# Ordering a hybrid attention and delta-rule block with another scheduler clock, from an inner context

## The chip, the cores and the metric

The kernel runs on one core of a Trainium2 chip, as one launch. The metric is the device time of that core in microseconds (us), and the lower one is better. A change is judged by the ratio of its time to that of the kernel before, measured in turns on the same chip.

The core has five engines that work side by side, each through a queue of its own, in order: PE (TensorE, the matmuls; its weight loads are a row of their own, PEld), DVE (VectorE), ACT (ScalarE), POOL (GpSimd) and SP (SyncE, which here issues nearly all DMAs).

## The reference

One layer of an encoder trunk, for two sequences of 256 and 512 rows with 1024 features. The input is normed and multiplied by one wide weight matrix; the product is cut into the inputs of two branches. One branch is attention with a difference of two softmaxes for each of 8 heads, the other a gated delta rule in both directions, in chunks of 64 in the reference. Gates merge the two, and a last matmul and norm follow. Cut to what matters:

```python
def trunk(x, norm_g, w_in, conv_w, lam_qk, diff_norm_g, a_log, dt_bias, gdn_norm_g, w_branch, w_out, final_g):
    h = rmsnorm(x, norm_g[l])
    proj = h @ w_in[l]
    q_a, k_a, v_a, z_a, qkv_b, z_b, a_b, b_b, gate = jnp.split(proj, SPLIT_POINTS, -1)
    y_a = diff_branch(q_a, k_a, v_a, z_a, lam_qk[l], diff_norm_g[l], lam_init, cos, sin)
    y_b = gdn_branch(qkv_b, z_b, a_b, b_b, conv_w[l], a_log[l], dt_bias[l], gdn_norm_g[l])
    gates = jax.nn.sigmoid(gate.astype(jnp.float32)).astype(x.dtype).reshape(B, S, 2, D)
    merged = gates[:, :, 0] * (y_a @ w_branch[l, 0]) + gates[:, :, 1] * (y_b @ w_branch[l, 1])
    x = x + merged @ w_out[l]
    return rmsnorm(x, final_g)

# attention branch: w = softmax(q1 k1) - lam * softmax(q2 k2); o = w @ v; rmsnorm; times silu(z)
# delta rule, for each direction and head, over chunks i:
    t = lax.linalg.triangular_solve(a + eye, eye, lower=True, unit_diagonal=True)   # a = strict(beta k k^T * decay)
    v_new = u_i - w_i @ state
    o = qg_i @ state + attn_i @ v_new
    state = state * gl_i + kd_i^T @ v_new
```

## The kernel before

Both sequences stand side by side, 768 columns in 6 chunks of 128. Values are float32; the large matmuls run with operands split into a high and a low part (`whi` and `wlo` for weights), so that each product is three matmuls.

*The weight stream.* The products with `w_in` and `w_branch` are cut into units of 128 output features. `load_split` (L155) loads a unit's weights on SP's queue (L157) into one of two buffers `raw` and splits them, on ACT (L152) and DVE (L153). The unit's body does 48 matmuls of 256 and 512 columns into `pa` and `pb` (L200) and then its epilogue: a convolution for the inputs of the delta rule (L394 to L408), a rotation for those of attention (L796 to L822), or a tanh for gates and z (L241 to L244, L289 to L291). `stream` (L185) hands out these matmuls in small steps.

*The work around it.* Four pairs of heads go through the delta rule (`gdn_pair`, L431): transposes of `kq` with norms (L448 to L464), values (L539, L540), decays (`decays`, L499: a gate, spread over a matrix, is summed by matmuls with a triangle, L526, and goes through an exp and a mask on POOL, L529), the inverse of the triangles (`inverse`), and six rounds of the scan, where DVE's `r` (L697) is the operand of the matmul at L708. Eight heads of attention follow, with a rope rotation, scores (L885), weights and a product with the values; each head ends in `finalize` (L295), with a power on POOL (L302), a scaling on DVE (L303) and transposes (L310). The last stages are the two branch products and `out_proj` (L990), which ends with the norm of each block of rows and its store (L1005 to L1014).

*What sets the order.* All of this is traced in one `TileContext`. Each traced instruction has a priority, counted up as it is traced. The weight stream is traced at priorities from 1000000 on, behind all else, except where a `fill` call asks for steps inline; `fill` calls also say how far the stream is traced at a point of the foreground. When the context closes, a list scheduler goes through the instructions with a simulated machine as its clock: at each point in that machine's time it gives each engine the ready instruction with the first priority, and that order becomes the engine's queue. Tile buffers are given out and semaphore waits are placed by the same pass. So the clock decides what counts as ready, and with it where the stream's matmuls stand between those of the foreground. The context before takes its time from the scheduler's default machine. All this happens while the kernel is built; on the chip each engine goes through its queue as it is.

`kernel` (L1096) opens the context and calls `tile_trunk` (L45), which holds all that is told above; L1110 is the line of the context's opening.

Of the kernel before, what the change touches and what calls it, by code (L numbers as in the profile page):

```python
# [41 lines left out]


@with_exitstack
def tile_trunk(  # L45
    ctx: ExitStack,
    tc: tile.TileContext,
    x_prompt, x_sample, norm_g, w_in, conv_w, lam_qk, diff_norm_g, a_log, dt_bias,
# [1027 lines left out]
    hes.close()  # L1076


# [1 line left out]
_INS = ["x_prompt", "x_sample", "norm_g", "w_in", "conv_w", "lam_qk", "diff_norm_g", "a_log", "dt_bias",  # L1080
        "gdn_norm_g", "w_branch", "w_out", "final_g"]
# [32 lines left out]
```

## Time and profile before

| | |
|---|---|
| median of 3 runs | 1220.1 us (1218.69 to 1220.44) |
| the profiled execution, its own time | 1219.2 us |
| its span, from the first to the last instruction | 1217.1 us |
| PE busy | 1186.3 us (97% of the span), 8015 matmuls |
| DVE, ACT, POOL busy | 754.4, 556.3, 132.0 us |
| mean granted clock of PE | 0.996 |

The profile is that of one execution. Its times are in us unless ns is said, counted from the first instruction; L12 is line 12 of the kernel; `out<-in` names the tile that an instruction writes and those that it reads. A granted clock of 1.00 is 2.4 GHz and one of 0.50 is 1.2 GHz. Matmuls are pipelined, so that neighbouring ones overlap in the list, and their ends are modelled. Idle time of an engine is put down to what ended it.

### The profile page before, as it was taken

How to read it: one execution, taken by the hardware profiler on the slowest of the kernel's cores; microseconds unless marked ns; L12 is line 12 of the kernel's file. 1: busy time of each engine (PE TensorE's matmuls, PEld its weight loads, DVE VectorE, ACT ScalarE, POOL GpSimd, SP SyncE). 2: the span in 40 equal slices, each digit the busy share in tenths (PEclk: the TensorE clock that was granted, in tenths of full speed). 3: DMA queues.
4: the chain of work that ended last, by engine and by line, in shares of the span. 5: the costliest groups of instructions: out<-in, count | busy, mean ns of one | idle time of the engine just before them, and what ended most of it. 6: DMA issues, size and time to landing. Idle time of an engine off the chain costs nothing. (4 is left out here: it accounts for less than half of the span.)

```text
span 1217.1 us, 20985 instructions
## 1 busy us (share of the span) xinstructions
PE 1186.3 (97%) x8015; PEld 1043.3 (86%) x8015; DVE 754.4 (62%) x1555; ACT 556.3 (46%) x1422; POOL 132.0 (11%) x242
## 2 busy tenths in 40 slices
PE   6999999999999999999999999999999999999997
PEld 5888889888888889888899889898898888888886
DVE  5778938667566855768354756767476645566332
ACT  6553546524672346722452545656365454332111
POOL 2132004301321013210000000000000000000000
PEclk9999999999999999999999999999999999999999
DMA  5123321244204340143425545353544548443131
GB/s 180 36 55 77 89 58 49 78 113 91 57 19 122 93 105 18 53 116 116 98 83 163 149 118 140 104 135 87 139 117 117 145 153 258 142 156 117 65 104 69
DMA packets 170647, 127.26 MB, mean 105 GB/s; under 512 B 53066, under 2 KB 147508, under 8 KB 170548
## 3 DMA queue, kind: packets, MB, share of 16 engines
q1 hardware_dynamic: 170416, 125.88, 37.2%
q8 instruction: 63, 1.03, 0.4%
q14 instruction: 36, 0.29, 0.1%
q10 hardware_dynamic: 132, 0.05, 0.0%
HBM read 83.43 MB, written 23.59 MB: 88 GB/s over the span
## 5 line engine op out<-in xcount | busy, mean ns | idle before, releaser
L200 PE MATMUL pb<-hT,whi 128*128 128x512 f32 x1152 | 430.8, 400 | 0.4 <-ACT hT L145 0.4
L200 PE MATMUL pa<-hT,whi 128*128 128x256 f32 x1152 | 317.3, 288 | 1.9 <-DVE gsp L243 1.9
L200 PEld LDWEIGHTS pb<-hT,whi 128*128 128x128 f32 x1152 | 216.1, 189 | 45.1 <-ACT hT L145 0.8
L200 PE MATMUL pb<-hT,wlo 128*128 128x512 f32 x576 | 228.9, 397 | 0.0
L200 PEld LDWEIGHTS pa<-hT,whi 128*128 128x128 f32 x1152 | 214.7, 190 | 6.3 <-DVE gsp L243 2.2
L152 ACT CAST whi<-raw 128x1024 fp32r<-128x1024 f32 x88 | 92.7, 1054 | 215.6 <-PE pb L200 206.5
L200 PE MATMUL pa<-hT,wlo 128*128 128x256 f32 x576 | 164.6, 286 | 0.0
L153 DVE TENSOR_TENSOR wlo<-raw,whi 128x1024 fp32r<-128x1024 f32 x88 | 107.7, 1224 | 78.1 <-ACT whi L152 77.9
L200 PEld LDWEIGHTS pb<-hT,wlo 128*128 128x128 f32 x576 | 108.7, 189 | 22.7
L200 PEld LDWEIGHTS pa<-hT,wlo 128*128 128x128 f32 x576 | 109.1, 189 | 1.5
L200 PE MATMUL pv<-vhi,hT 128*128 128x256 f32 x384 | 73.4, 287 | 0.3 <-ACT xp L796 0.3
L890 ACT ACTIVATE pw<-ps_sc,st 128x512 f32<-128x512 f32 (+1 forms) x96 | 58.2, 619 | 32.0 <-DVE st L888 31.9
L302 POOL TENSOR_TENSOR oss<-oss,mhalf 128x6 f32<-128x6 f32 x16 | 23.1, 1445 | 422.5 <-DVE oss L301 422.5
L404 DVE SCALAR_TENSOR_TENSOR kq<-xp,pcol,kq 128x258 f32<-128x258 f32 x96 | 56.2, 639 | 19.2 <-ACT kq L400 19.1
L200 PEld LDWEIGHTS pv<-vhi,hT 128*128 128x128 f32 x384 | 61.1, 191 | 1.2 <-ACT xp L796 0.6
L888 DVE TENSOR_REDUCE st<-ps_sc 128x1 f32<-128x512 f32 (+1 forms) x80 | 51.4, 682 | 10.2 <-PE ps_sc L886 9.9
L200 PE MATMUL pv<-vlo,hT 128*128 128x256 f32 x192 | 54.9, 286 | 0.0
L578 DVE TENSOR_TENSOR inv<-inv 96x31 f32<-96x31 f32 (+15 forms) x124 | 41.9, 338 | 17.5 <-ACT inv L556 14.2
L200 PE MATMUL pb<-yh,wlo 128*128 128x512 f32 x128 | 50.5, 396 | 0.0
L200 PE MATMUL pb<-yh,whi 128*128 128x512 f32 x128 | 50.4, 394 | 0.0
L200 PE MATMUL pb<-yl,whi 128*128 128x512 f32 x128 | 50.3, 393 | 0.0
L1004 PE MATMUL po<-hT,mh 128*128 128x512 f32 (+1 forms) x156 | 46.1, 378 | 0.3 <-DVE gth L949 0.3
(296 smaller groups left out, 2248.3 us busy)
## 6 DMA issues: line engine op xcount, KB each, us to landing
raw<-in_w_in SPq DMA_DIRECT2D x72, 512.0 KB, 4.1
xx<-xp SPq DMA_DIRECT2D x64, 192.0 KB, 3.5
raw<-in_w_branch SPq DMA_DIRECT2D x16, 512.0 KB, 4.0
gtd<-gsp SPq DMA_DIRECT2D x16, 384.0 KB, 2.7
th<-xp SPq DMA_DIRECT2D x64, 96.0 KB, 2.9
gth<-gtd SPq DMA_DIRECT2D x16, 384.0 KB, 4.2
vraw<-in_w_in SPq DMA_DIRECT2D x4, 1024.0 KB, 5.6
wor<-in_w_out SPq DMA_DIRECT2D x16, 256.0 KB, 3.5
```

The costliest lines, as they stand in the source:

```text
L152: nc.scalar.copy(whi, raw)
L153: nc.vector.tensor_tensor(out=wlo, in0=raw, in1=whi.bitcast(F32), op=ALU.subtract)
L200: nc.tensor.matmul(out, l_, r_, start=st, stop=sp)
L302: nc.gpsimd.tensor_tensor(out=oss[:, 0, :], in0=oss[:, 1, :], in1=mhalf[:, :NCH], op=ALU.pow)
L404: nc.vector.scalar_tensor_tensor(out=dst[:, a:b], in0=xp[:, w + a:w + b], scalar=cw(w), in1=dst[:, a:b], op0=ALU.mult, op1=ALU.add)
L578: nc.vector.tensor_tensor(out=tmp[:, :n, :w], in0=L[:, j + 1:, j:j + 1].to_broadcast(shp), in1=X[:, j:j + 1, :w].to_broadcast(shp), op=ALU ...
L888: nc.vector.tensor_reduce(out=st[:, c, :G], in_=ps.rearrange("p (g s) -> p g s", g=G), axis=AX.X, op=ALU.max, negate=True)
L890: nc.scalar.activation(pw[:, c, S * g_:S * g_ + S], ps[:, S * g_:S * g_ + S], AF.Exp, bias=st[:, c, g_:g_ + 1], accum_out=sums[:, c, i:i + 1])
L1004: nc.tensor.matmul(ps[:, :c1 - c0], a[:, ts_], b[:, cs], start=f, stop=l)
```

## The change

The function that traces the trunk is renamed to `trunk`. A new `tile_trunk` opens a section of the outer context that is scheduled as one piece (`tile_critical`), opens a second `TileContext` in it with the option `schedule_with_timeline_sim`, and traces the trunk in this inner context. With the option, the scheduler's simulated machine is the framework's timeline model in place of the default one. The body of the trunk, its priorities, its buffers and the call in `kernel` are as they were; the decays are still summed by matmuls (L526). The whole diff:

```diff
--- before.py
+++ after.py
@@ -42,7 +42,7 @@
 
 
 @with_exitstack
-def tile_trunk(
+def trunk(
     ctx: ExitStack,
     tc: tile.TileContext,
     x_prompt, x_sample, norm_g, w_in, conv_w, lam_qk, diff_norm_g, a_log, dt_bias,
@@ -1076,6 +1076,11 @@
     hes.close()
 
 
+def tile_trunk(tc, *args):
+    with tc.tile_critical(), tile.TileContext(tc.nc, schedule_with_timeline_sim=True) as inner:
+        trunk(inner, *args)
+
+
 # ---- launch: one core; inputs and outputs as the reference has them ----
 _INS = ["x_prompt", "x_sample", "norm_g", "w_in", "conv_w", "lam_qk", "diff_norm_g", "a_log", "dt_bias",
         "gdn_norm_g", "w_branch", "w_out", "final_g"]
```

## Rows read from the trace of the kernel before

**Rows 1.** The page: PE's busy time and share; granted clock in 40 slices, in tenths.
```profile
PE 1186.3 (97%) x8015; PEld 1043.3 (86%) x8015; DVE 754.4 (62%) x1555; ACT 556.3 (46%) x1422; POOL 132.0 (11%) x242
...
PEclk9999999999999999999999999999999999999999
```

**Rows 2.** Busy time by stretches: start:end, length, engines, PEclk, DMA share, GB/s.
```profile
0.00:40.00 40.00, 29.45 (x152) 24.21 (x153) 22.62 (x44) 24.31 (x44) 7.28 (x30) 1.00 0.48 150
...
1200.00:1217.00 17.00, 10.17 (x68) 9.13 (x66) 5.15 (x12) 2.11 (x8) 1.10 (x2) 0.88 0.16 62
```

**Rows 3.** What PE waited for: us in total, times, longest.
```profile
PE ps_par L116 <- DMA prow<-in_diff_norm_g: 7.4, 1, 7.4
...
PE ps_t L448 <- DVE kq L408: 2.1, 1, 2.1
PE pa L200 <- DVE gsp L243: 1.9, 1, 1.9
PE ps_yt L310 <- DVE o L303: 1.7, 1, 1.7
PE ps_x L708 <- DVE r L697: 1.4, 1, 1.4
...
PE ps_v L539 <- DVE vT L408: 0.2, 1, 0.2
```

**Rows 4.** Busy time by stretches, behind the stalls at 69 and 870 us.
```profile
70.00:72.00 2.00, 2.00 (x10) 1.91 (x10) 0.00 (x0) 1.22 (x8) 0.00 (x0) 0.50 0.80 235
72.00:74.00 2.00, 2.00 (x12) 1.77 (x11) 0.17 (x1) 1.54 (x9) 0.00 (x0) 0.75 0.03 8
...
872.00:874.00 2.00, 2.00 (x10) 1.90 (x10) 1.23 (x1) 0.56 (x1) 0.00 (x0) 0.50 1.03 247
874.00:876.00 2.00, 2.00 (x10) 1.76 (x9) 0.00 (x0) 0.22 (x1) 0.00 (x0) 0.72 0.94 276
```

**Rows 5.** Instructions in order: start, us, what, count, [idle before <- what ended it]; 69 us.
```profile
66.33 0.64 ACT L407 ACTIVATE th<-kq 128x512 f32<-128x512 f32 x1 [0.24 <-DVE kq L404]
...
67.06 1.21 DVE L153 TENSOR_TENSOR wlo<-raw,whi 128x1024 fp32r<-128x1024 f32 x1
...
68.77 1.02 DVE L408 SCALAR_TENSOR_TENSOR kq<-th,kq 128x258 f32<-128x258 f32 x2
...
69.24 0.44 PE L448 MATMUL ps_t<-ident,kq 128*128 128x128 f32 x2 [2.10 <-DVE kq L408]
69.44 0.44 PE L200 MATMUL pa<-hT,wlo 128*128 128x256 f32 x1
```

**Rows 6.** Instructions in order, around the stall at 192 us.
```profile
189.75 1.21 DVE L153 TENSOR_TENSOR wlo<-raw,whi 128x1024 fp32r<-128x1024 f32 x1
...
190.88 1.00 DVE L408 SCALAR_TENSOR_TENSOR vT<-th,vT 128x512 f32<-128x512 f32 x1
...
192.29 0.68 PE L708 MATMUL ps_x<-r,ma 128*128 128x128 f32 x4 [1.40 <-DVE r L697]
...
192.73 0.36 PE L200 MATMUL pa<-hT,whi 128*128 128x256 f32 x1
```

**Rows 7.** Instructions in order, before the stall at 870 us.
```profile
868.95 0.96 DVE L803 TENSOR_TENSOR xp<-xp,th 128x768 f32<-128x768 f32 x1
...
869.99 0.38 ACT L241 ACTIVATE th<-pa 128x256 f32<-128x256 f32 x1 [6.70 <-PE pb L200]
...
870.41 0.42 DVE L243 SCALAR_TENSOR_TENSOR gsp<-th,pa 128x256 f32<-128x256 f32 x1 [0.50 <-ACT th L241]
```

**Rows 8.** Instructions in order, before the stall at 227 us.
```profile
225.82 1.32 POOL L458 TENSOR_TENSOR nk<-nk,half 128x6 f32<-128x6 f32 x1 [5.76 <-DVE nk L459]
...
227.18 0.42 DVE L540 TENSOR_TENSOR v<-ps_v,nk 128x256 f32<-128x256 f32 x1 [1.14 <-POOL nk L458]
```

**Rows 9.** The tile `ee`, its step on POOL: count, ns min/median/max, first and last start.
```profile
L529 POOL TENSOR_SCALAR_AFFINE_SELECT ee<-ee x16: 862/868/5188, 56.8 to 481.2; 128x768 f32<-128x768 f32 x16
```

**Rows 10.** Groups of DVE by line: count | busy us, mean ns | idle before.
```profile
L697 DVE SCALAR_TENSOR_TENSOR r<-ps_s,NEGE,v 128x128 f32<-128x128 f32 x64 | 19.4, 345 | 12.6 <-PE ps_s L691 12.2
```

## The prediction, made before the changed kernel was run

> **What bounds the kernel now.** I read the views in this order: the busy times and the granted clock on the page, PE's busy time by stretches, the list of what PE waited for, and then the instructions in order of time around the three stalls that look like faults of order.
>
> PE is busy for 1186.3 of the 1217.1 us [rows 1]. No other engine comes near that, so the kernel is bound by how much PE has to do, and the change leaves PE's work as it is. The time can only move through what PE does not do: 1217.1 - 1186.3 = 30.8 us of idle time, and the time that PE runs at its lower clock.
>
> The idle time has three places. In the first 40 us PE is busy for 29.45, so 10.55 are idle; 7.4 of these are the wait for the parameters that the first transpose reads [rows 2, 3]. In the last 17 us PE is busy for 10.17, so 6.83 are idle: the norm of the last rows and their store, after PE's last matmul [rows 2]. That leaves 30.8 - 10.55 - 6.83 = 13.4 us for the 1160 us between. The list of PE's waits names fourteen stalls there, each a single one, the longest 2.1 us and the shortest 0.2 [rows 3]. Two of them cost more than they show. After the stall at 69 us the granted clock is 0.50 and then 0.75 in two stretches of 2 us, after the one at 870 us 0.50 and 0.72 [rows 4]: PE sat idle, fell to 1.2 GHz and came back to 2.4. That is 1.0 + 0.5 and 1.0 + 0.56, together 3.1 us. So **16.5 us** hang on the order in the middle (13.4 + 3.1), and that is all that a better order could give there.
>
> **The change part by part.** It neither adds nor removes an operation of the computation. It does two things: the whole trunk is traced in a second context inside a section of the first one, and that second context orders the instructions of every engine by another clock than before. Priorities, buffers, `fill` calls and the weight stream with its low priority stay as written.
>
> *The order.* The engines work their queues in the order that was fixed when the kernel was built; what the scheduler's clock decides is which instruction goes into a queue first when several could. Where it takes a result to be ready sooner than the chip has it, the instruction that needs it is queued too early, and what stands behind it waits too. Three stalls look like this.
>
> At 69 us PE waits for `kq` from L408. ACT's tanh for it had ended at 66.33 + 0.64 = 66.97, but L408 starts at 68.77: DVE had a weight split (L153, 1.21 us) and small steps of the norm ahead of it. 1.8 of the 2.1 us are this order, and the matmul behind the stalled pair is one of the weight stream, which needed nothing of it [rows 5]. At 192 us PE waits 1.40 us for `r` from L697; DVE ran a weight split and a conv step (L408) just before, and again the stream follows right behind the stall [rows 6]. At 870 us the tanh of a gate or z unit (L241) starts at 869.99, just after L803 has ended at 869.91: both use the one buffer `th`, and PE waits 1.87 us for the L243 behind it [rows 3, 7]. These three are 2.10 + 1.40 + 1.87 = 5.4 us, and the two drops of the clock follow two of them, 3.1. I take all 8.5 us as gone with a clock that is nearer to what the engines do.
>
> The rest, 16.5 - 8.5 = 8.0 us, I leave as it is. An example is the stall of 1.00 us at 227 us, which ends with L540 behind a step of POOL (L458, 1.32 us) on which DVE itself waited [rows 8]: a chain and not a queue, and any order has some of these. The bounds of this term: all 16.5 gone at one end; as much again added at the other, since a new order brings stalls that the trace before can't show. I take the value that the three stalls named give, since for these the rows show what stood in the way.
>
> At one place the Trainium skill speaks against so much. A step of POOL, L529, takes 868 ns in the median and once 5188 [rows 9], so durations depend on what runs beside them. SBUF — State Buffer, section "Who interferes with whom", states that a DVE instruction with two inputs in SBUF and a GpSimd instruction that reads SBUF exclude each other, and that the second is held up for the whole of the first; the spread in that row agrees. By that rule a clock that prices an instruction alone would still misplace the steps of DVE beside such a step of POOL; if that kept the stall at 69 us with its drop (2.1 + 1.5), the sum below would be 3.6 us higher.
>
> *The start and the end.* The waits of 10.55 and 6.83 us are chains of loads and of the last norm that no order shortens by much; I change nothing there. DMA issues, SP's queue included, are the same in number; their order moves with the rest, and is part of the bounds above.
>
> *The second context.* It has an entry and an exit of its own, within those of the first: its engines are drained once more and meet once more. The trace does not show one inside another. From below it costs nothing: it only adds, so a gain is excluded. From above I take what lies around the span now, 1219.2 - 1217.1 = 2.1 us, which holds one entry and one exit with all else that a launch needs. I take the middle, 1.0 us; nothing covers it, since PE has no work before or after the trunk.
>
> *The sum*, against the profiled execution's own 1219.2 us: 1219.2 - 8.5 + 1.0 = 1211.7. That execution lies 0.9 us below the median of the three runs, 1220.1, so on the scale of the median: **1212.6 us**.
>
> **The rivals.**
>
> *The margin goes (slower).* The present order is nearly free of stalls, and this may be because the old clock was wrong on the careful side: what PE needs is there before PE comes to it. Of the 64 steps `r` (L697), 32 hand-overs of two, one held PE up [rows 3, 10]. A clock that puts a matmul in the queue just when its operand is due leaves nothing for a step that comes late, and steps do come late (868 against 5188 ns [rows 9]). If one in four of the hand-overs of `r` held PE up as the one does, that alone would be 8 x 1.4 = 11.2 us, with clock drops behind some. I price this as twice the present stalls and drops: 16.5 more, 1220.1 + 1.0 + 16.5 = 1237.6. It decides as soon as the stalls and drops of the middle are more than 16.5 + 1.4 = 17.9 us, since 1220.1 + 1.0 + 1.4 = 1222.5 is 0.2% above. For it: so few stalls in so many hand-overs. Against it: behind the stalls that I looked at there was filler that could have gone first, and a scheduler that sees the delay would put it there.
>
> *No difference.* The new order is the old one in all that matters, or has other stalls of the same sum: 1220.1 + 1.0 = 1221.1. To this belongs the case that the change does not do what it says, and the inner context's order comes out as before. For it: the stream's low priority fills every gap under either clock, and 16.5 us are only 1.4% to begin with.
>
> *All of it gone.* The clock is good enough that the middle has no stall: 1220.1 - 16.5 + 1.0 = 1204.6. Against it: chains like that through POOL, and the loads in the last stage.
>
> **How the numbers follow.** The forecast has 0.44, the lost margin 0.30, no difference 0.20, all gone 0.06. A measurement of this kernel can tell about 0.2% (2.4 us) from no change. The forecast's own range goes from 1204.6 to 1217.7; with "all gone" it lies wholly on the faster side: 0.50. Same is 0.20, slower 0.30. The cases of both signs are far apart, so the range has to reach from the one to the other: from 1204, the end without any stall, to 1238, the price of the lost margin; perhaps 0.04 lie below and 0.13 above.
>
> **What would show it.** In the profile after, PE's busy time should be the same within what the lower clock adds, 1184 to 1188 us. The list of PE's waits should no longer have `kq` L408, `r` L697 and `gsp` L243 at their size, and no stretch between 40 and 1200 us should have a clock below 1. The first stretch should have about 10.5 us of idle time and the last about 7, with at most 2 us more before the first and after the last instruction. The step on the order is wrong if the middle has as much idle time as now, spread over many short waits: then the margin was what kept PE busy. The step on the second context is wrong if the idle time at either end grows by more than 2 us. The prediction as a whole is wrong if PE's own work changes, which nothing here would explain.

## The result, and the profile after

The changed kernel takes **1317.0 us** (median of 4 runs, 1315.8 to 1319.1) beside 1219.9 for the kernel before: a ratio of 1.080, 95% interval 1.078 to 1.082. It is slower by 97 us. The forecast was 1212.6 and the range ended at 1238; of the cases that stood in the prediction, the lost margin has the right sign and a sixth of the size.

The page of the kernel after, which answers to [rows 1]: busy times, and the granted clock in 40 slices.

```profile
PE 1213.0 (92%) x8015; PEld 1064.9 (81%) x8015; DVE 746.2 (57%) x1555; ACT 560.3 (43%) x1422; POOL 119.7 (9%) x242
...
PEclk9999999989999899898969999999999987999999
```

PE does the same 8015 matmuls. The span is 1315.0 us, so its idle time is 1315.0 - 1213.0 = 102.0 us where it was 30.8, and it is busy for 26.7 us longer for the same matmuls, with a clock that is no longer full: slices of 8, 7 and 6 tenths stand where all were 9. 71.2 of idle time and 26.7 of slower work are the 97.9 us between the two spans.

Where they lie is seen from PE's busy time by stretches. First the kernel before, from the first transpose of the first pair to the end of the last scan, then to the last head's last product, then to the last matmul (start:end, length, PE, PEld, DVE, ACT, POOL busy, PEclk, DMA share, GB/s); then the kernel after, the same three.

```profile
61.20:628.80 567.60, 560.55 (x4212) 493.35 (x4211) 381.65 (x933) 267.07 (x762) 102.22 (x193) 1.00 0.31 80
628.80:982.40 353.60, 350.54 (x2327) 316.93 (x2326) 222.42 (x387) 185.51 (x485) 13.33 (x9) 1.00 0.46 125
982.40:1210.20 227.80, 224.58 (x1207) 191.51 (x1206) 109.07 (x150) 66.40 (x108) 4.09 (x6) 1.00 0.42 134
```

```profile
0.00:40.00 40.00, 28.17 (x157) 23.99 (x158) 17.88 (x36) 21.65 (x39) 7.02 (x27) 1.00 0.45 137
...
83.30:715.10 631.80, 579.96 (x4210) 509.80 (x4209) 360.45 (x916) 267.92 (x757) 88.33 (x180) 0.95 0.28 73
715.10:1083.10 368.00, 350.62 (x2317) 318.68 (x2316) 228.21 (x388) 191.21 (x493) 12.26 (x9) 0.98 0.47 125
1083.10:1306.80 223.70, 210.90 (x1089) 175.53 (x1087) 99.85 (x138) 55.02 (x90) 4.08 (x6) 0.97 0.38 118
```

In the four pairs PE is idle for 631.80 - 579.96 = 51.8 us where it was 7.1, and 4210 matmuls take it 580 us where 4212 took 560.6: the mean clock there is 0.95. The heads have 17.4 us of idle time (3.1 before), the last stages 12.8 (3.2). The first 40 us answer to [rows 2]: 11.83 idle, 10.55 before. So the loss is not at the ends; it is spread over the middle, most of it in the pairs. The stretch of the pairs is longer by 64.2 us and that of the heads by 14.4. (Some of this is work done earlier: before the first transpose PE does 287 matmuls of the stream where it did 156, and the last stretch has 118 matmuls fewer.)

What PE waited for in the kernel after (us in total, times, longest) answers to [rows 3]:

```profile
PE ps_t L448 <- ACT kn L452: 14.0, 6, 3.2
PE ps_p L612 <- DMA XY<-sX: 12.8, 4, 10.5
PE ps_par L116 <- POOL rstd L135: 9.9, 1, 9.9
PE ps_yt L310 <- DVE o L303: 7.6, 1, 7.6
PE ps_y L661 <- ACT P L652: 6.7, 3, 2.9
PE ps_pv L919 <- ACT wT L910: 6.0, 5, 2.2
PE pa L200 <- DVE gsp L243: 5.6, 1, 5.6
...
PE ps_x L708 <- DVE r L697: 1.7, 8, 0.4
```

No single one is large; 27 kinds of wait share the sum. `ps_t`, `ps_p` and `ps_y` are steps of the pairs that take their operands from other engines. In the kernel before the same steps are there, but matmuls of the stream stood ahead of them in PE's queue, enough to fill the time. Here too few did at these places. Idle time spread over many short waits in the middle is the sign that the prediction named for a wrong step on the order.

### The profile page after: what moved, and what is told of

Read it like the earlier page. It is cut to its first block, busy times and chain, and to the rows that moved or that the text cites. A ratio compares the mean times of both kernels' runs of the same rounds, so it can differ in the third digit from the quotient of the medians.

```text
span 1315.0 us, 21029 instructions
## 1 busy us (share of the span) xinstructions
PE 1213.0 (92%) x8015; PEld 1064.9 (81%) x8015; DVE 746.2 (57%) x1555; ACT 560.3 (43%) x1422; POOL 119.7 (9%) x242
## 4 chain that ended last, share of the span: by engine, by line
PE 61%; DVE 12%; DMA 10%; ACT 7%; SPq 5%; issue 3%; POOL 0%; DVEq 0%; ACTq 0%; POOLq 0%
PE pb L200 25%; PE pa L200 13%; PE po L1004 5%; PE pv L200 2%; SPq L606 2%; ACT junk L450 2%; PE ps_pv L919 2%; DVE wlo L153 1%; PE ps_x L708 1%; PE ps_o L740 1%; DVE inv L580 1%; DVE inv L578 1%; DMA yr<-ybd 1%; ACT junk L300 1%; PE ps_ga L477 1%
## 5 line engine op out<-in xcount | busy, mean ns | idle before, releaser
L200 PE MATMUL pb<-hT,whi 128*128 128x512 f32 x1152 | 426.8, 400 | 0.0
L200 PE MATMUL pa<-hT,whi 128*128 128x256 f32 x1152 | 311.9, 287 | 5.6 <-DVE gsp L243 5.6
L200 PEld LDWEIGHTS pb<-hT,whi 128*128 128x128 f32 x1152 | 216.1, 189 | 46.3 <-DVE gsp L244 0.3
L200 PE MATMUL pb<-hT,wlo 128*128 128x512 f32 x576 | 229.9, 399 | 0.0
L200 PEld LDWEIGHTS pa<-hT,whi 128*128 128x128 f32 x1152 | 215.8, 192 | 10.1 <-DVE gsp L243 5.9
L200 PE MATMUL pa<-hT,wlo 128*128 128x256 f32 x576 | 164.5, 286 | 0.0
L153 DVE TENSOR_TENSOR wlo<-raw,whi 128x1024 fp32r<-128x1024 f32 x88 | 107.6, 1224 | 83.9 <-ACT whi L152 63.8
L200 PEld LDWEIGHTS pb<-hT,wlo 128*128 128x128 f32 x576 | 108.6, 188 | 23.0
L200 PEld LDWEIGHTS pa<-hT,wlo 128*128 128x128 f32 x576 | 110.5, 192 | 1.9
L890 ACT ACTIVATE pw<-ps_sc,st 128x512 f32<-128x512 f32 (+1 forms) x96 | 58.5, 615 | 46.8 <-DVE st L888 46.6
L200 PE MATMUL pv<-vhi,hT 128*128 128x256 f32 x384 | 71.9, 285 | 5.3 <-ACT vhi L152 5.3
L200 PEld LDWEIGHTS pv<-vhi,hT 128*128 128x128 f32 x384 | 60.1, 189 | 6.0 <-ACT vhi L152 5.5
L888 DVE TENSOR_REDUCE st<-ps_sc 128x1 f32<-128x512 f32 (+1 forms) x80 | 52.3, 683 | 14.0 <-PE ps_sc L886 13.8
L404 DVE SCALAR_TENSOR_TENSOR kq<-xp,pcol,kq 128x258 f32<-128x258 f32 (+1 forms) x96 | 54.2, 610 | 2.2 <-ACT kq L400 2.1
L200 PE MATMUL pv<-vlo,hT 128*128 128x256 f32 x192 | 54.1, 283 | 0.0
L200 PE MATMUL pb<-yl,whi 128*128 128x512 f32 x128 | 51.1, 399 | 0.0
L200 PE MATMUL pb<-yh,whi 128*128 128x512 f32 x128 | 50.9, 402 | 0.0
L200 PE MATMUL pb<-yh,wlo 128*128 128x512 f32 x128 | 50.8, 397 | 0.0
L810 ACT CAST hl<-xx 128x1536 fp32r<-128x1536 f32 x16 | 23.7, 1479 | 59.9 <-DMA xx<-xp 59.9
```

Source lines behind the costliest of these rows:

```text
L153: nc.vector.tensor_tensor(out=wlo, in0=raw, in1=whi.bitcast(F32), op=ALU.subtract)
L200: nc.tensor.matmul(out, l_, r_, start=st, stop=sp)
L404: nc.vector.scalar_tensor_tensor(out=dst[:, a:b], in0=xp[:, w + a:w + b], scalar=cw(w), in1=dst[:, a:b], op0=ALU.mult, op1=ALU.add)
L810: nc.scalar.copy(hl, xx)
L888: nc.vector.tensor_reduce(out=st[:, c, :G], in_=ps.rearrange("p (g s) -> p g s", g=G), axis=AX.X, op=ALU.max, negate=True)
L890: nc.scalar.activation(pw[:, c, S * g_:S * g_ + S], ps[:, S * g_:S * g_ + S], AF.Exp, bias=st[:, c, g_:g_ + 1], accum_out=sums[:, c, i:i + 1])
```

## Two ways in which steps come late, read in the trace of after

*Filler ahead of a product that is ready.* The kernel after, PE's instructions in order behind one `wT`, which ACT (first fence) has ready at 762.38 + 0.58 = 762.96 us:

```profile
762.38 0.58 ACT L910 COPY wT<-ps_wt 128x512 f32<-128x512 f32 x1
```

```profile
763.00 0.40 PE L200 MATMUL pb<-hT,whi 128*128 128x512 f32 x1
763.24 0.28 PE L200 MATMUL pa<-hT,whi 128*128 128x256 f32 x1
...
765.36 0.63 PE L200 MATMUL pb<-hT,whi 128*128 128x512 f32 x2
766.62 0.66 PE L310 MATMUL ps_yt<-ident,o 128*128 128x128 f32 x4 [0.63 <-DVE zt L312]
...
768.04 1.05 PE L919 MATMUL ps_pv<-v,wT 128*128 128x128 f32 x8
```

The product comes 5.1 us after its operand; 3.0 of them, to 765.99, are matmuls of the stream. I measured this hand-over over the whole trace, from the end of each L910 to the start of the first L919 that reads it, and counted the stream's matmuls (L200) that start in between. Before, the median of 40 is 0.18 us with none in between; after, it is **2.88 us with 17**. In the scan the means go from 0.30 to 1.50 us for `xd` (L727) to L737, and from 0.23 to 1.18 for `xn` (L730) to L740.

*A step that waits for a DMA at the head of a queue.* The kernel after, ACT in order of time, a few us later:

```profile
772.99 1.47 ACT L810 CAST hl<-xx 128x1536 fp32r<-128x1536 f32 x1 [9.25 <-DMA xx<-xp]
774.36 0.68 ACT L890 ACTIVATE pw<-ps_sc,st 128x512 f32<-128x512 f32 x1
```

and PE in the same stretch:

```profile
775.19 0.51 PE L885 MATMUL ps_sc<-hl 128*128 128x512 f32 x1 [2.26 <-ACT pw L890]
```

ACT stood for 9.25 us before L810, a step of the rope rotation that needs a DMA. The exponential of the current head (L890) stood behind it in the queue. Its own operand, the maximum from L888 on DVE, had been ready at 770.6, so it came 3.8 us late, and PE waited 2.26 us for it. Over the whole run ACT waited 59.9 us, 15 times, at L810 for `xx`; before it was 19.0, 7 times. These are waits of ACT, and PE pays for a part of them only: the whole stretch of the heads is 14.4 us longer.

Which of these makes the loss, and what the second context has to do with it, is what the experiments were for.

## The experiments

All ratios are to the kernel before, measured beside the run. The table gives PE's busy time in the profiled execution and its idle time (span less busy).

| run | us | ratio (95%) | PE busy | PE idle |
|---|---|---|---|---|
| before | 1219.9 | 1 | 1186.3 | 30.8 |
| after | 1317.0 | 1.080 (1.078-1.082) | 1213.0 | 102.0 |
| inner_only | 1223.9 | 1.004 (1.003-1.005) | 1186.6 | 35.5 |
| flag_only | 1288.9 | 1.057 (1.055-1.060) | 1209.6 | 77.7 |
| flag_cold | 1315.7 | 1.079 (1.076-1.082) | 1215.5 | 100.4 |
| before_cold | 1222.6 | 1.003 (1.002-1.005) | 1184.9 | 34.3 |
| all_of_after | 1287.9 | 1.056 (1.053-1.059) | 1206.3 | 78.6 |
| pe_of_before | 1289.4 | 1.057 (1.056-1.059) | 1201.5 | 85.6 |
| pe_of_after | 1307.9 | 1.073 (1.070-1.075) | 1218.3 | 89.1 |
| others_of_before | 1364.9 | 1.121 (1.118-1.123) | 1227.0 | 138.3 |
| rope_held | 1243.9 | 1.020 (1.017-1.023) | 1193.8 | 49.6 |
| split | 1304.3 | - (one run) | 1224.0 | 78.5 |
| pin | 1366.3 | 1.121 (1.117-1.125) | 1214.7 | 146.7 |
| early16 | 1315.7 | 1.079 (1.076-1.082) | 1216.3 | 95.8 |
| pace48 | 1307.1 | 1.073 (1.070-1.075) | 1214.7 | 90.0 |
| pace8 | 1272.0 | 1.044 (1.041-1.047) | 1202.2 | 70.1 |
| lump16 | 1253.1 | 1.029 (1.027-1.031) | 1201.5 | 51.5 |
| late16 | 1244.7 | 1.021 (1.019-1.024) | 1192.8 | 50.8 |
| late96 | 1271.0 | 1.044 (1.042-1.045) | 1204.5 | 64.5 |
| three_fixed | 1216.8 | 0.999 (0.998-1.000) | 1186.2 | 29.0 |

The theories of the first four runs: A, the new clock puts a number of the stream's matmuls into PE's queue ahead of a foreground matmul that it does not yet hold ready; B, the new clock prices each hand-over too long, and fills that time; C, the nesting is the cause, whatever the clock; D, the loss is in the order of DVE and ACT. Later ones are named where they are tested.

### The two halves of the change

inner_only has the second context with the old clock:

```diff
-    with tc.tile_critical(), tile.TileContext(tc.nc, schedule_with_timeline_sim=True) as inner:
+    with tc.tile_critical(), tile.TileContext(tc.nc) as inner:
```

> The inner context and its section alone, with the scheduler's clock of before. Theory A (the order by the new clock costs it: stream matmuls stand in PE's queue ahead of foreground ones that are already due) and theory B (the new clock takes each hand-over between engines for longer than it is) both say: nothing of the 97 us; 1219 to 1223 us, PE idle about 31 us, and the second context's own price can be read from the two ends. Theory C (the section or the second context costs it, by its barriers or its semaphores): most of the 97 us, about 1317.

flag_only is the kernel before with the new clock and no second context:

```diff
-    with tile.TileContext(nc) as tc:
+    with tile.TileContext(nc, schedule_with_timeline_sim=True) as tc:
```

> The new clock alone, given to the one outer context, with no inner one. A and B: the whole loss, 1310 to 1320 us, with the same waits of PE as in the changed kernel (ps_t behind kn some 14 us, ps_p behind XY some 13). C: near 1220.

Measured: +4.6 us for the context alone (1.0038), +70 for the clock alone (1.0574), and 97 for both. So C is out as the main cause; but A and B wanted all of the 97 from the clock, and 4.6 and 70 are not 97. The built programs and the traces tell that this is no matter of order: in each of the five queues inner_only has the order of the kernel before, and flag_only that of the kernel after, instruction by instruction. Some 27 us lie between two programs with the same queues.

### What the second context costs: longer DMA issues

The two traces differ in the DMA issues (and in 40 instructions that the kernel after has more, 21029 against 20989). L606, one of the burst of small DMAs of the inverse, as SP's queue issues it (minimum, median and maximum in ns, first and last start in us), in flag_only and then in after:

```profile
L606 SPq DMA_DIRECT2D ma<-sY x64: 303/439/1898, 173.1 to 665.8; - x64
```

```profile
L606 SPq DMA_DIRECT2D ma<-sY x64: 556/604/1726, 177.0 to 684.3; - x64
```

In the built programs, 419 of the 547 DMA instructions on SP carry a mark for a short form when the trunk is traced in the outer context, and none does in the inner one. The framework has a switch for it, so that it can be tried without a second context. (The pinning of a queue's order, by edges between its instructions, is shown under all_of_after, where it is also seen to cost nothing by itself.) flag_cold is flag_only with its queues pinned to their own order, and the switch off:

```diff
+    nc.dge_precook = False
     with tile.TileContext(nc, schedule_with_timeline_sim=True) as tc:
         tile_trunk(tc, *args)
+        pin_order(tc)
```

> The new clock without the inner context, each of the five queues pinned to the order that flag_only has, and one switch off: the short form in which the framework may write a DMA instruction for its queue (in the traces the issues of L606 take 439 ns in the median in flag_only and 604 in after, though the queues of the two have one order). If these longer issues are what the inner context costs on top of the new order: 1317 us (1313 to 1320), with the median issue of L606 at 604 ns and waits of PE on ps_p for XY of about 12.8 us. If the section itself, its drain or its later start costs it: 1289 to 1292, whatever the issues take.

before_cold is the kernel before with the same switch off; its order stays the same.

> The kernel before with the one switch of flag_cold, so that no DMA instruction has the short form; its queues have the same order. If the longer issues are all that the inner context costs: the ratio of inner_only, 1.004 (1.0025 to 1.0051). If a part of those 4.6 us is the section's own: less, 1.000 to 1.002.

flag_cold takes 1315.7 us, as the kernel after within the intervals, and its L606 the 604 ns; before_cold has 1.0033, which overlaps the 1.0038 of inner_only. flag_cold has 20989 instructions, so the 40 more are not what costs. So the longer issues are what the second context costs, under either order; a part of some 2 us for its own entry and exit is within the intervals. Under the old order most of the price lies at the start: in inner_only PE waits longer for the parameters that the first transpose reads (7.4 us before [rows 3], and 10.4 in before_cold), and its pairs have no more idle time than before (6.8 us).

```profile
PE ps_par L116 <- DMA prow<-in_diff_norm_g: 10.2, 1, 10.2
```

Where it costs more under the new order shows in the first pair. SP's queue and ACT around one burst, flag_only:

```profile
173.14 8.95 SPq L606 DMA_DIRECT2D ma<-sY  x16
182.19 1.28 SPq L291 DMA_DIRECT2D gtd<-gsp  x1
...
186.05 0.39 ACT L289 ACTIVATE gsp<-pa 128x256 f32<-128x256 f32 x1 [1.77 <-DMA gtd<-gsp]
186.81 0.87 ACT L652 COPY P<-ps_p 128x384 f32<-128x384 f32 x2
```

and after, same queues, same instructions:

```profile
176.95 11.63 SPq L606 DMA_DIRECT2D ma<-sY  x16
188.69 0.55 SPq L291 DMA_DIRECT2D gtd<-gsp  x1
...
191.64 0.38 ACT L289 ACTIVATE gsp<-pa 128x256 f32<-128x256 f32 x1 [5.17 <-DMA gtd<-gsp]
192.40 0.87 ACT L652 COPY P<-ps_p 128x384 f32<-128x384 f32 x2
```

The burst of 16 takes 2.7 us longer. Behind it stands the store of a gate; a step of ACT waits for its buffer, and behind that in ACT's queue stands `P`, which PE needs. Over the whole run `ps_y` waits 6.7 us for `P` in after and 1.0 in flag_only, and `ps_p` waits 12.8 us for `XY` and 7.6. Of the 24.3 us of idle time that after has more than flag_only, 16.2 lie in the pairs. In the lists of before and inner_only PE has no wait at `ps_y` or `ps_p`: in the old order other matmuls stand over these stretches. The Trainium skill, Perfetto Trace Analysis, section "What 'DMA-bound' means", names the issuing engine's sequencer, its track solid with DMA slices, among the things that can bind a DMA-bound kernel. This kernel as a whole is bound by PE, but the trace agrees for this burst: SP issues for 10.97 of the 11.63 us, and 41 GB/s are moved meanwhile, where the kernel before has stretches with 276 [rows 4].

### The order alone makes the other 70 us

all_of_after is the kernel before, old clock and outer context, with an edge of order from each instruction to the next in all five queues, as the kernel after has them. The edges only say which is queued first; they add no wait.

```diff
+def pin_order(tc):
...
+        for a, b in zip(order[:-1], order[1:]):
+            tc.add_manual_dep(mine[b], mine[a].name,
+                              mybir.DependencyInfo(mybir.DependencyClass.NoSync, mybir.DependencyReason.DATA),
+                              reason="order of a queue")
...
         tile_trunk(tc, *args)
+        pin_order(tc)
```

> The kernel before, with its old clock and without the inner context, all five queues pinned to the order that they have in the changed kernel; DMAs have the short form. If the option acts only through the order of the queues: as flag_only, 1286 to 1292 us. If the new clock does anything beside that (buffers given out otherwise, other waits): off by more than 5 us.

1287.9 us, beside 1288.9 for flag_only: to within about a microsecond the new clock acts through the order of the queues and through nothing else, and the edges by themselves cost nothing. The next three ask which queue. They use the same edges for some of the queues; the rest is ordered anew by the clock that is named, around what is pinned.

pe_of_before has the new clock and PE's queue as before:

> The new clock without the inner context; only PE's queue is pinned, to the order that it has in the kernel before; DVE, ACT, POOL and SP are ordered by the new clock. Theory A (the loss is in PE's order: stream matmuls ahead of foreground matmuls): 1216 to 1226 us, PE busy 1184 to 1190. Theory D (the loss is in the order of DVE and ACT, conv steps within the inverse loop): 1250 to 1290.

pe_of_after has the old clock and PE's queue as after:

> The kernel before with its old clock; only PE's queue is pinned, to the order that it has in the changed kernel; the other queues are ordered by the old clock. Theory A: as slow as the new clock alone, 1280 to 1295 us. Theory D: 1220 to 1245.

others_of_before has the new clock and the queues of DVE, ACT and POOL as before:

> The new clock without the inner context; the queues of DVE, ACT and POOL are pinned to their order in the kernel before, PE and SP are ordered by the new clock. With pe_of_before at 1289 neither half alone is safe. If the order of DVE and ACT is the half that matters: 1219 to 1228 us. If the new clock still spends the filler in lumps on PE (from wT to ps_pv a median of 2 us or more, some 17 stream matmuls): 1245 to 1290.

Neither A nor D holds through the three. Giving PE its old order back gains nothing in sum (1289.4, at the upper end of what D had); PE's new order with the old clock for the rest is worse than the new order whole (1307.9, above what A had and far above D); and giving the others theirs back makes it far worse (1364.9, above both cases). So no queue alone carries the loss. These are not halves of two schedules put together, since what is not pinned follows: in pe_of_before an instruction of DVE stands on average 2.3 places from its place in the kernel before, in flag_only 23; and in others_of_before PE's queue is neither that of before nor that of flag_only. That queues made in one piece fit each other better is a reading of this, not a thing shown.

But pe_of_before tells more by stretches. The pairs and the heads, the two stretches as above, first of flag_only, then of pe_of_before:

```profile
81.70:695.20 613.50, 577.90 (x4211) 508.59 (x4209) 361.25 (x916) 268.63 (x756) 87.23 (x180) 0.96 0.29 75
695.20:1060.50 365.30, 349.58 (x2317) 318.19 (x2315) 228.60 (x389) 191.69 (x493) 12.27 (x9) 0.98 0.46 126
```

```profile
62.90:647.70 584.80, 565.46 (x4212) 496.42 (x4211) 379.20 (x933) 268.73 (x761) 97.13 (x193) 0.99 0.30 77
647.70:1050.50 402.80, 360.06 (x2329) 323.38 (x2327) 223.39 (x385) 186.82 (x485) 12.48 (x9) 0.97 0.41 110
```

With PE's old order the pairs take 584.8 us (567.6 before, 613.5 in flag_only), and their idle time falls from 35.6 us to 19.3 (7.1 before). They end at 647.7 in place of 695.2; a part of these 47.5 us is no gain, since flag_only has done 2448 matmuls of the stream by then and before 2324. The heads are another matter: 402.8 us where before has 353.6 and flag_only 365.3, with 42.7 us of idle time.

### Steps that wait for a DMA

In pe_of_before the queues of DVE and ACT differ little from before (the 2.3 places above; 1.0 for ACT), but in the heads the steps of the rotation (L801 to L803 and L822 on DVE, L810 on ACT) have moved ahead of the maximum and the weights (L888, L890, L902). One place in its trace, instructions in order:

```profile
749.04 1.48 ACT L810 CAST hl<-xx 128x1536 fp32r<-128x1536 f32 x1 [7.04 <-DMA xx<-xp]
...
750.54 1.75 DVE L822 TENSOR_TENSOR hl<-xx,hl 64x1536 fp32r<-64x1536 f32 x1 [5.99 <-ACT hl L810]
...
752.33 2.48 DVE L888 TENSOR_REDUCE st<-ps_sc 128x1 f32<-128x512 f32 x4
...
757.99 1.41 DVE L902 SCALAR_TENSOR_TENSOR pw<-pw,st 128x512 f32<-128x512 f32 x2
...
758.88 0.45 PE L908 MATMUL ps_wt<-ident,pw 128*128 128x128 f32 x1 [6.45 <-DVE pw L902]
```

The scores that L888 reduces were there at 748.8. DVE could not take them: L822 stood at the head of its queue for 5.99 us, waiting for ACT, which waited for a DMA, so that L888 starts 3.6 us late; further steps of the rotation (L801 to L803) stand ahead of L902. At the end of this chain PE waits 6.45 us. rope_held adds one set of edges to pe_of_before: each such step is queued no earlier than behind the instruction that it follows in the kernel before (96 edges on DVE, 16 on ACT).

```diff
         pin_order(tc)
+        hold(tc)
```

> pe_of_before with one set of order edges more: no step of the rotation that waits for a DMA (L801, L802, L803, L822 on DVE, L810 on ACT) may be queued before the instruction that it follows in the kernel before. Theory E (the new clock takes DMAs to land sooner than they do, so that these steps stand at the head of their queues and block what PE needs): the stretch from the last scan to the last head falls from 403 us to 355 to 370, the time from 1289 to 1240 to 1260. If something else in these queues blocks PE: 1275 or more.

1243.9 us, 45 less, within what was expected. The same two stretches of rope_held, and then ACT's wait at L810 in it (it was 50.9 us, 15 times, in pe_of_before):

```profile
63.00:647.90 584.90, 565.77 (x4212) 496.47 (x4211) 379.27 (x933) 268.88 (x761) 97.22 (x193) 0.99 0.30 77
647.90:1008.10 360.20, 352.13 (x2327) 316.57 (x2326) 222.97 (x385) 185.78 (x485) 12.49 (x9) 1.00 0.46 123
```

```profile
ACT hl L810 <- DMA xx<-xp: 22.3, 7, 5.5
```

The heads are back to 360.2 us, and the pairs have not moved. So with PE's old order, these steps are 42.6 of the 49.2 us that the heads lost. That is the price under PE's old order alone: in flag_only, with the new one, the heads lost 11.7 us in all. That the new clock holds DMAs to land sooner than they do would explain why it puts the steps there; its times were not read, so this is argued and not shown.

### The stream's matmuls on PE

Theory A says how the foreground matmuls come late: a number of stream matmuls is committed ahead of each. split halves those of 512 columns, so that a number of them takes less time.

```diff
-                    nc.tensor.matmul(out, l_, r_, start=st, stop=sp)
+                    if r_.shape[-1] == 512:
+                        nc.tensor.matmul(out[:, :256], l_, r_[:, :256], start=st, stop=False)
+                        nc.tensor.matmul(out[:, 256:], l_, r_[:, 256:], start=False, stop=sp)
+                    else:
+                        nc.tensor.matmul(out, l_, r_, start=st, stop=sp)
```

> As changed, but every stream matmul of 512 columns is made as two of 256, so that PE has the same columns in more and shorter instructions (0.117 us each in place of 0.117 and 0.236). Theory A in the form that the clock lets a number of instructions stand in PE's queue: as many stream matmuls as now stand between the end of wT and the matmul that reads it (median 17), so the delay falls from about 2.9 to about 2.0 us, and the time falls, 1260 to 1300 us. Theory B: the delay stays at 2.9 us with about 25 matmuls in it, and the time at 1310 to 1325.

From `wT` to `ps_pv` the median is 18 matmuls and 2.28 us (after: 17 and 2.88). The number stayed and the delay fell, as A has it and B has not. PE is busy 11.0 us longer for the more matmuls and idle 23.5 us less than in after; the time of the one run, 1304.3 us, lies between the ranges of A and B and decides nothing.

pin puts the first matmul of each step of the stream behind all that was traced before it on PE, by the framework's own call for this:

```diff
+                    if j == 0:
+                        tc.keep_in_program_order(mm)
```

> As changed, but the first matmul of every step of the stream may not stand in PE's queue ahead of a PE instruction that was traced before it (an edge on the queue's order alone, no wait). A (and B): what costs is the place of the stream in PE's queue, so the stream matmuls between wT and its matmul fall from 17 to under 10, and at least half of the 97 us come back: 1225 to 1268 us. Theory D (the order in the queues of DVE and ACT costs it, with the convolution's steps inside the triangles' inverse): PE's order is not the point, and the time stays above 1290.

1366.3 us, a miss. `ps_p` now waits 67.8 us, 8 times, for the DMA of `XY`: the stream, which covers the DMAs of the inverse, may no longer go ahead of anything. And the number between `wT` and `ps_pv` is still 16, where A wanted it under 10, so pin did not test A. The order as traced is no better guide than the clock.

early16 is flag_only with PE's queue pinned, and each foreground matmul of the pairs and heads moved up to 16 stream matmuls to the front:

> The new clock without the inner context; PE's queue is pinned to the order of flag_only with one edit: each foreground matmul of the pairs and of the attention heads stands up to 16 stream matmuls earlier. Theory A (a foreground matmul comes about 16 stream matmuls after its operand is there, and this is what slows the foreground): from wT to ps_pv the median falls from 2.88 to under 1 us, and the time to 1225 to 1250. If the loss comes from how far the stream as a whole runs ahead and not from the single hand-overs: 1275 or more. If 16 is too many, new waits of PE for the operands: above 1289.

1315.7 us, with 18 matmuls and 3.18 us from `wT` to `ps_pv`: a miss for A, above 1289 as the last of the three cases has it. The edit moves all foreground matmuls alike, so the number between two of them stays and A is not tested by it. What it shows is that being 16 ahead as such is worth nothing here.

The number between them can be read from the order in which PE ran. I counted the runs of stream matmuls between two foreground ones:

| | runs | of 1 to 3 | of 4 to 11 | of 12 to 24 | over 24 |
|---|---|---|---|---|---|
| before | 227 | 110 | 61 | 28 | 28 |
| after, flag_only | 174 | 36 | 41 | 66 | 31 |
| pace48 | 179 | 35 | 54 | 60 | 30 |
| pace8 | 188 | 28 | 76 | 58 | 26 |

The old order gives nearly half of its gaps one to three matmuls (110 of 227); in the new one the commonest run has 12 to 24 (66 of 174). The stream is the same 4800 matmuls, so gaps that get more than they need leave others without. That the long runs lose the time is theory L. It has a rival in PE's order, S: the new clock takes the stream early as a whole (287 of its matmuls before the first pair's transposes, where before has 156), and it runs dry at the end of the pairs (288 in the fourth pair, where before has 543). pace48 and pace8 tell them apart. They are flag_only with a cap: each 48th, or each 8th, matmul of the stream is not queued before the foreground matmul that it follows in the kernel before.

```diff
+    for s, f in _PACE:
+        tc.add_manual_dep(mine[s], mine[f].name,
+                          mybir.DependencyInfo(mybir.DependencyClass.NoSync, mybir.DependencyReason.DATA),
+                          reason="pace of the stream")
```

> The new clock without the inner context, all queues ordered by it, with a cap on the stream's lead: each 48th of its matmuls may not be queued before the foreground matmul that it follows in the kernel before (99 such edges). Theory S (the lead is the loss): 1225 to 1250 us. Theory L (the long runs are the loss): 1265 to 1290, with the hand-over from wT to ps_pv still near 2.9 us in the median.

> As pace48 with an edge at each 8th matmul of the stream (599 edges), so that the runs of the stream between two foreground matmuls are held closer to those of the kernel before too. Theory L: clearly below pace48, 1225 to 1255 us. Theory S: within 10 us of pace48. Theory M (the queues of the new clock do not fit PE's old order, as in pe_of_before, whatever the stream does): 1280 or more.

pace48 takes the lead away (191 matmuls before the first pair, 536 in the fourth) and leaves most of the long runs: 1307.1 us, 18 slower than flag_only. The idle time of the pairs does not shrink but moves: in flag_only 17.2 of 36 us lie in the fourth pair, in pace48 10.6 of 41. So S is out as the main cause. pace8, which holds the stream closer to the old order, takes 1272.0: 35 us less than pace48 and 17 less than flag_only. M, by which 1280 or more was due, is out.

The order of the two is theory L's, but L is not shown by them. pace48 lies above L's range (1265 to 1290), and L's condition for it failed: from `wT` to `ps_pv` the median is 1.48 us and not near 2.9, and in pace8 it is 1.35, hardly less. pace8 did not come down to the 1255 that L had as its upper end. Runs of 12 and more are 90 in pace48 and 84 in pace8, a small difference for 35 us; what else the closer cap does was not taken apart.

Three more start from the kernel before and its old clock, with one edit to PE's queue in the pairs: lump16 puts the stream in blocks of 16, late16 and late96 put the foreground 16 or 96 stream matmuls later.

> The kernel before, PE's queue pinned to its own order with one edit: within the four pairs, the stream's matmuls stand in blocks of 16 between the foreground's, in place of the few at each step as before (each foreground matmul of the pairs moves behind at most 15 more of the stream); the other queues by the old clock. Theory L (the new clock spends the filler in lumps of some 17 matmuls, about 2.9 us, at hand-overs that need 0.3 to 0.5 us, and none is left for the others): PE's idle time between 61 us and the end of the fourth pair rises from 7 to 25 to 45 us, the time is 1245 to 1270. If lumps as such do no harm: below 1228, idle under 12.

> As late96 with a shift of 16 stream matmuls in place of 96. If what late96 lost comes from the lead, it goes with the dose: 1220 to 1230 us. If it comes from editing one queue alone, the same as late96 or lump16: 1245 to 1275.

> The kernel before, PE's queue pinned to its own order with one edit: the foreground matmuls of the pairs stand 96 stream matmuls (two units) later, so that the stream runs ahead by about as much as under the new clock (287 of its matmuls against 156 at the first transpose); the number between two foreground matmuls stays as it was nearly everywhere; the other queues by the old clock. Theory L: the lead alone costs little, 1219 to 1230 us, idle of PE in the pairs under 15. Theory S (the stream's lead is the loss, since the stream runs dry at the end of the pairs): 1245 or more, with most of the new idle time in the fourth pair.

lump16: 1253.1 us, 35 more than before and within L's range, with 21.9 us of idle time in the pairs (7.1 before; 25 was expected at least). late96: 1271.0, with 31.5 us idle in the pairs; that is above L's range (1219 to 1230) and in S's, but only 10 of the 31.5 lie in the fourth pair, where S would have most. late16: 1244.7, already 25 more for a small shift, just under the range that it had for the cost of editing one queue alone. Where its time goes is seen in the list of what PE waited for:

```profile
PE pa L200 <- DVE wlo L153: 9.3, 2, 6.8
PE pa L200 <- ACT whi L152: 4.5, 2, 2.7
```

These 13.8 us are the stream's own matmuls, which now stand ahead of the split of their weights; lump16 has 1.0 of that. So the two lose in different ways, and neither is a clean test of the runs. What the three show together is how tight the old order is: with the other queues ordered anew by the old clock, a shift of PE's by 16 matmuls still costs 25 us.

### Were the three stalls worth what the prediction took?

three_fixed is the kernel before with all queues pinned and three edits on DVE's: L408 of `kq` ahead of the weight split at 67 us, two steps `r` ahead of the split and a conv step at 190 us, L303 behind L803 at 866 us.

> The kernel before, all five queues pinned to their own order with three edits on DVE's, one for each stall that the prediction wanted gone: L408 of kq ahead of the weight split at 67 us, the first two steps r (L697) ahead of the weight split and the conv step at 190 us, and L303 behind L803 at 866 us. If these stalls and the clock drops behind them are worth what the prediction took (8.5 us, of which the third edit can give only about half of its part): 1212 to 1215 us. If what is saved there is lost at the next wait: 1218 to 1222.

1216.8 us, ratio 0.9987 (0.9977 to 0.9998): some 1.6 us gained of the 8.5 that the prediction took (the third edit could give only about half of its part); 1212 to 1215 was expected if the stalls were worth that. What PE waited for in it:

```profile
PE ps_x L708 <- ACT xd L727: 3.2, 1, 3.2
...
PE ps_t L448 <- ACT kn L452: 0.9, 1, 0.9
...
PE ps_t L448 <- DVE kq L408: 0.6, 2, 0.4
```

`kq` has fallen from 2.1 to 0.6, and `r` and `gsp` are gone from the list [rows 3]. In their place stand 3.2 us for `xd`, which was not among the waits before, so most of what was saved is lost at a later step. (`kn` is no new wait: its line in the kernel before reads as follows.) No version tried beats the kernel before by more than the 0.2% that a measurement can tell.

```profile
PE ps_t L448 <- ACT kn L452: 1.0, 1, 1.0
```

### What stays open

The 70 us of the order are shown as a whole. Of its parts, the steps at the head of DVE's and ACT's queues are shown to cost 45 us under PE's old order, but in flag_only the heads lost only 11.7 us. The closer cap on the stream is worth 35 us between pace48 and pace8; that the length of the runs is what makes these is argued. The parts don't add up, and how the 70 us of flag_only divide between the two stays open, most of all for the pairs, where 45.9 of them lie. That the clock lets a fixed number of matmuls be queued ahead fits the 17 and 18, but the clock itself was not looked into.

## Why the prediction was wrong, point by point

*PE's work bounds the kernel and is not changed.* The count held, 8015 matmuls. That PE's busy time would be 1184 to 1188 did not: 1213.0. The prediction looked for the lower clock behind two stalls only, some 1.5 us each [rows 4]; with idle time all over the middle the mean clock in the pairs is 0.95, and each us of new idle time came with 26.7 / 71.2 = 0.4 us of slower matmuls.

*16.5 us hang on the order, "and that is all that a better order could give there".* As a bound of a gain nothing speaks against it; three_fixed got 1.6 of the 8.5. **The step that failed is the next one: the loss was bounded by the same number** ("as much again added at the other end"). all_of_after shows a loss of 70 us by the order alone, four times the 16.5. The idle time of a tuned order says what is left to win. What there is to lose is what the order covers: 4800 of the 8015 matmuls are stream, laid into the gaps of a foreground whose steps go to other engines and back all the time. A row for that stood in the trace of before, L200 alone in the stretch of the pairs (length, PE, PEld, PEclk, DMA share, GB/s):

```profile
61.20:628.80 567.60, 411.31 (x2167) 334.10 (x2167) 1.00 0.31 80
```

For up to 411 of these 568 us PE is at work only because there is filler for it. The prediction looked at the fourteen places where the cover failed and not at the cover.

*The three stalls go, -8.5.* `kq` is gone from the list of after. `r` is on it 8 times with 1.7 us in sum, `gsp` once with 5.6 us where it had 1.9. The new clock did not remove such faults, it made others; and three_fixed shows that removing them by hand gives 1.6 us, since a new wait of 3.2 us comes in.

*The second context, 0 to 2.1 us, taken 1.0.* 4.6 under the old order, 27 under the new. The sum held an entry and an exit, since the prediction took it that a second context only adds. It changes how 419 of SP's 547 DMA instructions are built. The sign that was named for it was more than 2 us of idle time at either end. In the kernel after it did not come: the first 40 us have 1.3 more, and most of the cost lies in the pairs. Under the old order it did: in inner_only the first 40 us have 12.8 us of idle time, 2.3 more than before.

*The margin goes (the rival).* Its mechanism is nearest to what happened. Its count came out by luck: one in four of the 32 hand-overs of `r` [rows 10] was to hold PE up, and 8 did. Its price did not: 0.2 us each and not 1.4, and the time went at other hand-overs, most of them of the inverse, the transposes and the heads. The argument against it was that there was filler that could have gone first, "and a scheduler that sees the delay would put it there". It did put it there, 17 matmuls at a time at the hand-over of `wT`; how much of the loss that makes is open.

*A clock nearer to what the engines do.* This carried the sign, and no row stood behind it: the trace of before says nothing of the new clock. The chance of 0.5 for faster rested on what the option is called.

*POOL's long step [rows 9].* In the kernel after L529 takes 857 ns at the least, 864 in the median and 2937 at most. The four that take over 900 ns start before 86 us, and each runs beside a step of DVE (L517, L404, L408 or L153), as the 5188 ns of before do beside L517. No wait of PE in the kernel after is put down to it, and no run set the two steps apart.

## What to carry to other kernels

Before changing what sets the order of a tuned kernel, ask what the order covers, not only what it leaves idle: the idle time tells what can be won, and the filler that stands in the foreground's gaps tells what can be lost. Two things to look for in a trace of a new order are runs of filler that are longer than the gap needs, and steps that wait for a DMA at the head of an in-order queue with ready work behind them; the second was shown here to cost time, the first was not shown apart. When a wrapper "only" nests a kernel, compare the durations of the instructions too, the DMA issues among them, and not their order alone.

## What the runs showed of the hardware

One and the same DMA takes its queue a different time to issue, by the form in which it was built: L606 439 against 604 ns in the median, the store of a gate (L291) 319 against 451 at the least. (The first number of each pair is flag_only's, the second that of the kernel after.) Those of the rotation take 591 (L799) and 589 (L808) in either, and they are the 128 that carry no mark in the outer context either. In a burst of 16 the difference is 2.7 us (8.95 against 11.63), and the DMAs behind the burst on the queue start later by it.
